# Upper and lower weight parts of the MLPs made per 2048-column unit in three buffers instead of per 1024-column half in six

## The chip, the cores and the metric

The kernel runs on one core of one Trainium2 chip. The metric is the device time of one execution in microseconds (us). A core has a matrix engine (PE, with its weight loads shown apart as PEld), a vector engine (DVE), an activation engine (ACT), GpSimd (POOL) and SyncE (SP), which here only issues transfers. Each engine works through its own queue in order. They wait for each other by semaphores.

## What is computed

The reference is a trunk of two layers on 256 tokens of width 2048, float32. Layer 0 mixes tokens by a convolution module, layer 1 by latent attention, and each mixer is followed by an MLP:

```
def sq_relu_mlp(h, w1, w2):
    return jnp.square(jax.nn.relu(h @ w1)) @ w2

for layer in range(DEPTH):
    h = rms_norm(x, norm_mixer_g[layer])
    x = x + (conv_module(h, ...) if layer % 2 == 0 else mla(h, ...))
    h = rms_norm(x, norm_mlp_g[layer])
    x = x + sq_relu_mlp(h, mlp_w1[layer], mlp_w2[layer])
return rms_norm(x, final_norm_g)
```

In the MLPs `w1` is 2048 x 8192 and `w2` 8192 x 2048, so their weights are 256 of the kernel's loads of 1 MB.

## The kernel before

**Products in two parts.** PE multiplies in a short float format (`F32R`). So each float32 operand is made into an upper part `hi`, a rounded copy, and a lower part `lo`, the rest, and a product is upper by upper, upper by lower and lower by upper. For weights, ACT writes `hi` (an activation with Copy, L443) and DVE then writes `lo = raw - hi` (a subtraction, L444). `lo` of a tile therefore always waits for `hi` of it. `split_into` (L442) issues both.

**The units of an MLP.** Each load of 128 x 2048 float32 into a tile `raw` is a unit. There are three kinds.
- An *up unit* ("T", `up_unit`, L515) is one block of 128 columns of `w1`. It is split as two halves of 1024 columns. PE runs 8 products with `hi` of the first half, 8 and 8 with `lo` of both halves, and 8 with `hi` of the second (L535 upper, 512 columns wide; L531 lower, 256 wide). Then ACT copies the result from PSUM to the tile `U` (L543).
- A *seven-product pair* ("S", `seven_unit`, L697) replaces the eight block products of two by two blocks of `w2` by seven, by Strassen's scheme in Winograd's form. DVE first makes four sums of the weight blocks: `T` (two at once, L735), and one after the other the two halves of `V` (L742, L747), the first from `T`, the second from the first. Four chunks follow: `one` (512 columns of `raw`), `two` (1024 of `raw`), `t13` (`T`), `t24` (`V`), each split and then used by 3 or 6 matmuls (L209, L210, L211).
- A *plain pair* ("O", `plain_unit`, L671) is two chunks of 1024 columns with 12 matmuls each.

**Activations of a pair.** When both up units (b = 0 and b = 1) of a pair are done, five steps are queued in a list `todo`: `add` (DVE, L558, the two halves of `U` added), an empty one, `square` (ACT: relu L563, then square L566), `forms` (DVE, three small subtractions L577, L580, L581) and `part` (ACT L443 writes `sh`, DVE L444 writes `sl`). The tiles are `W`, or `U` itself for a plain pair.

**The order.** `stream` (L446) writes out by hand, in the order of the program, what each engine does. Before chunk n is run on PE it prepares chunks up to n + 5 (`WB` = 6 buffers of 1024 columns for `hi`, six for `lo`). Ahead of each chunk that it prepares it takes one step from `todo`, or two if more than four are waiting (L459 to L479). The sums `T` are made one chunk earlier (`ahead`). An MLP has four parts (`q`). First come the 16 up units of part 0; then for parts 0 to 2 two stretches of 16 units each, in the orders `STSTSTOSTSTSTSTT` and `TSTSTSTOSTSTSTST` (L57), in which the pairs of one part and the up units of the next alternate; last, the 16 pairs of part 3 without up units. Here a *cycle* means the two stretches of one part: 14 S, 16 T and 2 O. There are six cycles in the kernel.

**Neighbours.** All stages share the `hi` and `lo` buffers of one pool, `wpool`; the convolution and the attention fill them through `split_half` (L168). The steps of the scheduler around an MLP are also of use below: `xs` adds (L362 and L609) put results onto the residual stream, `xt` (L224, L231) is the transposed input of the next products, and between the convolution and MLP 0 stands the preparation of the rotary tables: ACT issues the load of the positions (L1249), DVE works out the angles (L1251 to L1291), ACT takes sine and cosine (L1296, L1299).

Of the kernel before, what the change touches and what calls it, by code (L numbers as in the profile page):

```python
# [18 lines left out]
P = 128  # L19
D = 2048  # L20
KC = D // P
T = 2
# [18 lines left out]
LO_GAP = 64  # L41
# [4 lines left out]
WB = 6  # L46
LOOK = WB // 2 - 1
# [40 lines left out]
def trunk_kernel(  # L88
# [32 lines left out]
    small = ctx.enter_context(tc.tile_pool(name="small", bufs=1))  # L121
    psum, psum_cx = {}, [ExitStack()]
# [45 lines left out]
    def split_half(raw, h, eng):  # L168

        _, nj, cols = raw.shape  # L170
        js = slice(h * nj // 2, (h + 1) * nj // 2)
        hi = wpool.tile([P, nj // 2, cols], F32R, tag="hi", name=nm("hi"), bufs=WB)
        lo = wpool.tile([P, nj // 2, cols], F32R, tag="lo", name=nm("lo"), bufs=WB)
        nc.scalar.activation(hi, raw[:, js, :], AF.Copy)  # L174
        eng.tensor_tensor(lo, raw[:, js, :], hi.bitcast(F32), op=ALU.subtract)  # L175
        return hi, lo
# [256 lines left out]
    class Chunk:  # L433
        def __init__(self, prep, run, after=(), now=None, ahead=None):
            self.prep, self.run, self.after, self.now, self.ahead = prep, run, after, now, ahead
# [10 lines left out]
    def stream(chunks, todo, blocked, pool):  # L446
# [12 lines left out]
        def next_step():  # L459
            if todo and (todo[0] not in blocked or blocked[todo[0]]()):  # L460
                todo.pop(0)()

        def prep():
            n = done[0]
            if n == len(chunks):
                return
            done[0] += 1
            unit, c = chunks[n]
            unit.chunks[c].prep(raws[unit], parts.setdefault(unit, {}))
            if done[0] < len(chunks):  # L470
                unit, c = chunks[done[0]]
                if unit.chunks[c].ahead is not None:
                    unit.chunks[c].ahead(raws[unit])
                unit, c = chunks[n]
            if c == unit.last_read:
                start(homes[unit])
# [3 lines left out]
        for n, (unit, c) in enumerate(chunks):  # L480
            chunk = unit.chunks[c]
            while done[0] < min(n + WB, len(chunks)):
                for _ in range(2 if len(todo) > 4 else 1):
                    next_step()
                prep()
            if done[0] == len(chunks):
                for fn in todo[: 2 if n < len(chunks) - 1 else None]:
# [9 lines left out]
    def mlp(layer, ssq, next_gain, finish=None, before=None, last_w1=None):  # L497
# [11 lines left out]
        def up_units(hs, q, p, extra):  # L509
# [5 lines left out]
            def up_unit(b):  # L515
                ps = []

                def chunk(h):
                    def prep(raw, parts):
                        parts[h] = [a.rearrange("p a (j n) -> p (a j) n", n=P) for a in hi_lo(2, LO_GAP - 8)]  # L520
                        split_into(parts[h], raw[:, 8 * h : 8 * h + 8, :])

                    def run(parts):
                        if not ps:
                            ps.append(acc_tile())
                        wh, wl = parts.pop(h)
                        for low in (h, 1 - h):
                            for j in range(8):
                                k = 8 * h + j
                                if low:  # L530
                                    nc.tensor.matmul(  # L531
                                        ps[0][:, :S], wl[:, j, :], alternate(xh(k)), start=False, stop=False
                                    )
                                else:
                                    nc.tensor.matmul(  # L535
# [1301 lines left out]
```

## Time and profile before

| what | us |
|---|---|
| median of 3 runs (lowest, highest) | 1875.48 (1875.22, 1875.72) |
| the profiled execution's own time | 1875.54 |
| its span | 1873.8 |
| PE busy in the span | 1826.8 |
| DVE busy | 1645.1 |
| ACT busy | 1200.4 |

A span is the time from the first to the last instruction; the execution's own time is 1.7 us longer. In a timeline row stand the start and the duration in us, the engine, the source line, the operation, what it writes from what it reads, the shape, the count of like instructions merged into the row and, in brackets, how long the engine was idle before it and what ended that wait. Groups give the busy time and the mean duration of one in ns. Instructions of one engine overlap at their ends: the distance from one start to the next can be shorter than the duration.

### The profile page before, as it was taken

To read this page: it belongs to the slowest core of one execution; us is meant where nothing else is said; L and a number is where in the kernel's file an instruction comes from. 1 tells how busy PE (TensorE), PEld (TensorE's weight loads), DVE (VectorE), ACT (ScalarE), POOL (GpSimd) and SP (SyncE) were. 2 spreads that over 40 slices of the span, in tenths; PEclk is the share of its full clock that TensorE was granted. 3 is DMA by queue.
4 is the path that set the end of the run, shared out by engine and by line. 5 is a ranking of instruction groups with operands and counts; after the bars stand their busy time and mean duration, and the time that the engine had idled before them with its cause. 6 is when DMAs were issued, how large, how long until landed. Compare 5 with 4: busy or idle time off the path is not lost.

```text
span 1873.8 us, 28470 instructions
## 1 busy us (share of the span) xinstructions
PE 1826.8 (97%) x10768; PEld 1650.0 (88%) x10768; DVE 1645.1 (88%) x2370; ACT 1200.4 (64%) x1716; POOL 222.7 (12%) x185
## 2 busy tenths in 40 slices
PE   7999999999999999999999999999999999999998
PEld 7999888998888888888899998899888898888887
DVE  5999975789999999999977666668999999999987
ACT  5556764767666666767566665566666766666754
POOL 5999400000000000000001420000000000000000
PEclk9999999999999999999999999999999999999999
DMA  8767366857667667766646445776666776766763
GB/s 237 197 185 195 119 210 170 239 176 215 193 212 209 202 205 215 209 211 214 217 151 201 116 146 192 209 195 180 202 198 208 216 210 186 218 208 203 226 240 112
DMA packets 407113, 367.62 MB, mean 196 GB/s; under 512 B 15416, under 2 KB 351936, under 8 KB 406720
## 3 DMA queue, kind: packets, MB, share of 16 engines
q1 hardware_dynamic: 405952, 363.63, 64.9%
q8 instruction: 84, 1.38, 0.3%
q10 hardware_dynamic: 1024, 2.17, 0.3%
q14 instruction: 53, 0.43, 0.1%
HBM read 363.68 MB, written 2.10 MB: 195 GB/s over the span
## 4 chain that ended last, share of the span: by engine, by line
PE 70%; DVE 19%; ACT 5%; issue 4%; DMA 1%; POOL 0%; SPq 0%; ACTq 0%; DVEq 0%
PE acc L535 18%; PE acc L211 13%; PE acc L209 13%; PE acc L210 13%; PE acc L531 10%; DVE sum L996 7%; DVE lo L444 5%; ACT hi L443 2%; DVE lo L175 1%; DVE T L735 1%; PE acc L219 1%; PE acc L220 1%; PE acc L218 1%; PE acc L274 1%; DVE U L558 1%
## 5 line engine op out<-in xcount | busy, mean ns | idle before, releaser
L444 DVE TENSOR_TENSOR lo<-raw,hi 128x1024 fp32r<-128x1024 f32 (+1 forms) x512 | 569.8, 1121 | 65.9 <-ACT hi L443 65.5
L443 ACT ACTIVATE hi<-raw 128x1024 fp32r<-128x1024 f32 (+1 forms) x512 | 477.0, 968 | 46.1 <-PE acc L210 44.0
L535 PE MATMUL acc<-xt,hi 128*128 128x512 f32 x2048 | 478.2, 379 | 0.5 <-ACT hi L443 0.5
L535 PEld LDWEIGHTS acc<-xt,hi 128*128 128x128 f32 x2048 | 377.2, 189 | 48.7 <-ACT hi L443 0.9
L211 PE MATMUL acc<-lo,sh 128*128 128x512 f32 x930 | 355.4, 382 | 7.5 <-DVE lo L444 7.5
L209 PE MATMUL acc<-hi,sh 128*128 128x512 f32 x930 | 353.4, 380 | 0.0
L210 PE MATMUL acc<-hi,sl 128*128 128x512 f32 x802 | 304.0, 379 | 0.0
L531 PEld LDWEIGHTS acc<-xt,lo 128*128 128x128 f32 x2048 | 249.2, 192 | 11.0 <-DVE lo L444 4.2
L531 PE MATMUL acc<-xt,lo 128*128 128x256 f32 x2048 | 251.5, 275 | 2.7 <-DVE lo L444 2.1
L211 PEld LDWEIGHTS acc<-lo,sh 128*128 128x128 f32 x930 | 175.7, 189 | 43.0 <-DVE lo L444 18.2
L174 ACT ACTIVATE hi<-raw 128x1024 fp32r<-128x1024 f32 (+2 forms) x184 | 179.7, 1005 | 43.2 <-PE acc L210 39.4
L209 PEld LDWEIGHTS acc<-hi,sh 128*128 128x128 f32 x930 | 175.8, 189 | 23.7
L443 ACT ACTIVATE hi<-V 128x1024 fp32r<-128x1024 f32 x94 | 99.3, 1057 | 142.3 <-DVE V L747 133.0
L175 DVE TENSOR_TENSOR lo<-raw,hi 128x1024 fp32r<-128x1024 f32 (+2 forms) x118 | 132.7, 1144 | 63.2 <-ACT hi L174 63.0
L443 ACT ACTIVATE hi<-T 128x1024 fp32r<-128x1024 f32 x94 | 99.2, 1055 | 118.6 <-DVE T L735 107.0
L210 PEld LDWEIGHTS acc<-hi,sl 128*128 128x128 f32 x802 | 151.6, 189 | 21.5
L996 DVE SCALAR_TENSOR_TENSOR sum<-ub,w_dw,sum 128x256 f32<-128x256 f32 x392 | 159.1, 486 | 6.1 <-ACT sum L952 5.1
L175 POOL TENSOR_TENSOR lo<-raw,hi 128x1024 fp32r<-128x1024 f32 x66 | 156.6, 2387 | 22.7 <-ACT hi L174 20.6
L218 PE MATMUL acc<-xt,hi 128*128 128x256 f32 x512 | 142.2, 278 | 0.0
L219 PE MATMUL acc<-xt,hi 128*128 128x256 f32 x512 | 140.9, 275 | 0.5 <-DVE xt L231 0.5
L220 PE MATMUL acc<-xt,lo 128*128 128x256 f32 x512 | 141.0, 275 | 0.0
L444 DVE TENSOR_TENSOR lo<-V,hi 128x1024 fp32r<-128x1024 f32 x94 | 115.0, 1223 | 6.3 <-ACT hi L443 3.0
(275 smaller groups left out, 2760.2 us busy)
## 6 DMA issues: line engine op xcount, KB each, us to landing
raw<-in_mlp_w SPq DMA_DIRECT2D x256, 1024.0 KB, 6.1
raw<-in_conv_w_pw SPq DMA_DIRECT2D x64, 512.0 KB, 5.5
raw<-in_conv_w_pw SPq DMA_DIRECT2D x16, 1024.0 KB, 5.1
raw<-in_mla_w_o SPq DMA_DIRECT2D x16, 1024.0 KB, 5.5
raw<-in_mla_w_kv_up SPq DMA_DIRECT2D x8, 1024.0 KB, 5.4
raw<-in_mla_w_in SPq DMA_DIRECT2D x8, 576.0 KB, 3.8
raw<-in_mla_w_in SPq DMA_DIRECT2D x4, 1024.0 KB, 7.5
raw<-in_mla_w_q_up SPq DMA_DIRECT2D x16, 256.0 KB, 5.0
```

Source lines behind the costliest of these rows:

```text
L174: nc.scalar.activation(hi, raw[:, js, :], AF.Copy)
L175: eng.tensor_tensor(lo, raw[:, js, :], hi.bitcast(F32), op=ALU.subtract)
L209: nc.tensor.matmul(ps, sh, mh, start=start, stop=False)
L210: nc.tensor.matmul(ps, sl, mh, start=False, stop=False)
L211: nc.tensor.matmul(ps, sh, ml, start=False, stop=stop)
L218: nc.tensor.matmul(ps, wh, alternate(th), start=start, stop=False)
L220: nc.tensor.matmul(ps, wl, alternate(th), start=False, stop=stop)
L443: nc.scalar.activation(parts[0], src, AF.Copy)
L444: nc.vector.tensor_tensor(parts[1], src, parts[0].bitcast(F32), op=ALU.subtract)
L531: nc.tensor.matmul(ps[0][:, :S], wl[:, j, :], alternate(xh(k)), start=False, stop=False)
L535: nc.tensor.matmul(ps[0], wh[:, j, :], xhl(k).rearrange("p (g a b) -> p g b a", g=2, a=2), start=k == 0, stop=k == KC - 1,)
L996: nc.vector.scalar_tensor_tensor(out=out, in0=ubs[c][:, w : w + S], scalar=tap(c, w), in1=pcs[c], op0=ALU.mult, op1=ALU.add)
```

## The change

- `hi` and `lo` of an MLP have three buffers (`MB` = 3) of 2048 columns, in place of six of 1024. The total size is the same. They are taken from a pool of their own, closed and opened anew between the stages (`open_parts`), so that the first tiles of a stage lie over the last tiles of the stage before.
- An up unit and a plain pair are one chunk each: one ACT instruction and one DVE instruction of 2048 columns.
- A seven-product pair is two chunks: `alone` (1536 columns of `raw`) and `summed` (2048 columns). All four sums lie in one tile `TV`; `sums` makes the first three, `alone` the fourth.
- `stream` prepares chunks up to n + 2. It takes a batch of min(3, (length of `todo` + 1) // 2) steps ahead of each preparing function.
- The order of the matmuls is as it was. The shift of `lo` by `LO_GAP` is gone.

```
-    def hi_lo(n, at=0):
-        hi = wpool.tile([P, n, NB], F32R, tag="hi", name=nm("hi"), bufs=WB)
-        lo = wpool.tile([P, n * NB + LO_GAP], F32R, tag="lo", name=nm("lo"), bufs=WB)
-        return [hi, lo[:, at : at + n * NB].rearrange("p (a b) -> p a b", b=NB)]
+    def hi_lo(n):
+        return [
+            parts_pool[0].tile([P, 4, NB], F32R, tag=c, name=nm(c), bufs=MB)[:, :n, :] for c in ("hi", "lo")
+        ]
...
         def next_step():
-            if todo and (todo[0] not in blocked or blocked[todo[0]]()):
-                todo.pop(0)()
+            for _ in range(min(3, (len(todo) + 1) // 2)):
+                if todo and (todo[0] not in blocked or blocked[todo[0]]()):
+                    todo.pop(0)()

         def prep():
...
+            for i, fn in enumerate(unit.chunks[c].prep):
+                next_step()
+                fn(raws[unit], parts.setdefault(unit, {}))
+            if c == 0:
                 start(homes[unit])
...
-            while done[0] < min(n + WB, len(chunks)):
-                for _ in range(2 if len(todo) > 4 else 1):
-                    next_step()
+            while done[0] < min(n + MB, len(chunks)):
                 prep()
...
+                def prep(raw, parts):
+                    parts["w"] = hi_lo(4)
+                    split_into(parts["w"], raw.rearrange("p (a j) n -> p a (j n)", a=4))
...
+                def sums(raw, parts):
+                    x = raw.rearrange("p j (b n) -> p (j b) n", b=2)
+                    tv.append(mp.tile([P, 4, NB], F32, tag="TV", name=nm("TV"), bufs=1))
                     nc.vector.tensor_tensor(
+                        tv[0][:, 0:2, :], x[:, 0:1, :].broadcast_to([P, 2, NB]), x[:, 1:3, :], op=ALU.add
                     )
+                    nc.vector.tensor_tensor(tv[0][:, 2, :], tv[0][:, 0, :], x[:, 2, :], op=ALU.add)
+
+                def alone(raw, parts):
+                    x = raw.rearrange("p j (b n) -> p (j b) n", b=2)
+                    nc.vector.tensor_tensor(tv[0][:, 3, :], tv[0][:, 2, :], x[:, 3, :], op=ALU.add)
+                    parts["alone"] = hi_lo(3)
+                    split_into(parts["alone"], x[:, 1:4, :])
+
+                def summed(raw, parts):
+                    parts["summed"] = hi_lo(4)
+                    split_into(parts["summed"], tv[0])
...
+        open_parts(f"parts_m{layer}")
```

Three places show how the instructions move. In the changed program the lines are others: `split_into` is L452 (ACT) and L453 (DVE), the copy to `U` is L540, `add` L552, relu L557, square L560, `forms` L571 to L575, the sums L727, L730 and L734.

On ACT, in a stretch where S and T alternate, behind an up unit with b = 1, before:

```order
L443 ACTIVATE hi_6015<-raw_5864 128x1024
L543 ACTIVATE U_5946<-acc_5998 128x512
L443 ACTIVATE hi_6037<-raw_5864 128x1024
L563 ACTIVATE U_5946<-U_5946 128x2x256
L566 ACTIVATE W_6050<-U_5946 128x512
L443 ACTIVATE hi_6054<-raw_5887 128x512
```

The same place on ACT now (`hi_5918` is of the sums, `hi_5962` of the next up unit):

```order
L452 ACTIVATE hi_5918<-TV_5896 128x2048
L540 ACTIVATE U_5879<-acc_5922 128x512
L557 ACTIVATE U_5879<-U_5879 128x2x256
L560 ACTIVATE W_5958<-U_5879 128x512
L452 ACTIVATE hi_5962<-raw_5804 128x2048
```

Before, the `hi` that DVE needs next stood between the copy to `U` and the relu; now it stands behind relu and square.

On DVE, at the same place, before:

```order
L444 TENSOR_TENSOR lo_6016<-raw_5864,hi_6015 128x1024
L558 TENSOR_TENSOR U_5946<-U_5946 128x2x256
L444 TENSOR_TENSOR lo_6038<-raw_5864,hi_6037 128x1024
L735 TENSOR_TENSOR T_6041<-raw_5887 128x1024
L444 TENSOR_TENSOR lo_6055<-raw_5887,hi_6054 128x512
L742 TENSOR_TENSOR V_6042<-T_6041,raw_5887 128x512
```

And on DVE now, from the sums of a seven-product pair to the `forms`:

```order
L727 TENSOR_TENSOR TV_5896<-raw_5742 128x1024
L730 TENSOR_TENSOR TV_5896<-TV_5896,raw_5742 128x512
L734 TENSOR_TENSOR TV_5896<-TV_5896,raw_5742 128x512
L453 TENSOR_TENSOR lo_5901<-raw_5742,hi_5900 128x1536
L453 TENSOR_TENSOR lo_5919<-TV_5896,hi_5918 128x2048
L552 TENSOR_TENSOR U_5879<-U_5879 128x2x256
L453 TENSOR_TENSOR lo_5963<-raw_5804,hi_5962 128x2048
L571 TENSOR_TENSOR W_5958<-W_5958 128x256
```

Each sum now stands right behind the one that it reads; one instruction lies between the fourth sum and `lo` of the sums; and `lo_5963` follows the `add` with nothing between.

On DVE, at the passage from MLP 0 to the attention, before (`lo_9923` to `lo_9948` are of the first weights of the attention, 576 columns each):

```order
L175 TENSOR_TENSOR lo_9923<-raw_9916,hi_9922 128x576
L175 TENSOR_TENSOR lo_9927<-raw_9916,hi_9926 128x576
L175 TENSOR_TENSOR lo_9933<-raw_9918,hi_9932 128x576
L231 SCALAR_TENSOR_TENSOR xt_3456<-acc_9793,vecs,xt_3456 128x256 x2
L231 SCALAR_TENSOR_TENSOR xt_3456<-acc_9802,vecs,xt_3456 128x256 x2
L175 TENSOR_TENSOR lo_9937<-raw_9918,hi_9936 128x576
L231 SCALAR_TENSOR_TENSOR xt_3457<-acc_9827,vecs,xt_3457 128x256 x2
L231 SCALAR_TENSOR_TENSOR xt_3457<-acc_9836,vecs,xt_3457 128x256 x2
L175 TENSOR_TENSOR lo_9948<-raw_9920,hi_9947 128x576
L609 SCALAR_TENSOR_TENSOR xs<-acc_9593,r_480_3873,xs 128x512
```

And now:

```order
L603 SCALAR_TENSOR_TENSOR xs<-acc_8873,r_480_3876,xs 128x512
L603 SCALAR_TENSOR_TENSOR xs<-acc_8847,r_480_3876,xs 128x512
L603 SCALAR_TENSOR_TENSOR xs<-acc_8843,r_480_3876,xs 128x512
L603 SCALAR_TENSOR_TENSOR xs<-acc_8890,r_480_3876,xs 128x512
L1398 MEMSET scratch 64x256 x2
L1401 MEMSET scratch 1x64
L1402 MEMSET scratch 1x64
L1401 MEMSET scratch 1x64
L1402 MEMSET scratch 1x64
L184 TENSOR_TENSOR lo_9182<-raw_9175,hi_9181 128x576
```

The first `lo` of the attention (`lo_9923`, now `lo_9182`) stood ahead of the last four `xs` adds of the MLP, and stands behind them and the memsets now.

More of the change, by code (lines that the diff above doesn't have):

```diff
@@ L40 @@
 PAD_RIGHT = 40
-LO_GAP = 64
 PAD_XT = 16
@@ L46 @@
 WB = 6
+MB = 3
 LOOK = WB // 2 - 1
@@ L556, in add @@
+                after = [add, lambda: None, square, forms, part] + extra if b == 1 else []
+                return Unit(
+                    rows(w1, 0, KC, ((q * NPAIR + p) * 2 + b) * P, P), KC, [Chunk([prep], run, after)]
+                )
             def add():
@@ L737, in sums @@
                     )
-                def one(raw, parts):
-                    parts["one"] = hi_lo(1)
-                    split_into(parts["one"], x[0][:, 1:2, :])
-                    nc.vector.tensor_tensor(tt[1][:, 0, :], tt[0][:, 0, :], x[0][:, 2, :], op=ALU.add)
-                def two(raw, parts):
-                    parts["two"] = hi_lo(2)
-                    split_into(parts["two"], x[0][:, 2:4, :])
-                    nc.vector.tensor_tensor(tt[1][:, 1, :], tt[1][:, 0, :], x[0][:, 3, :], op=ALU.add)
```

161 lines of the change are left out of this document (65 added, 96 removed).

## The prediction

> **What bounds the kernel now.** I began with the page's first part, to see which engines are near their limit over the whole span.
>
> ```profile
> span 1873.8 us, 28470 instructions
> ...
> PE 1826.8 (97%) x10768; PEld 1650.0 (88%) x10768; DVE 1645.1 (88%) x2370; ACT 1200.4 (64%) x1716; POOL 222.7 (12%) x185
> ```
>
> PE is busy for 97%, so all the time to be won on it is 47 us; DVE follows with 88%. Means over unlike stages say little, so I went to one cycle (14 S, 16 T, 2 O), from the lower products of one up unit to those of the unit in the same place one part later.
>
> ```profile
> core 0: us, PE busy (x) PEld busy (x) DVE busy (x) ACT busy (x) POOL busy (x), PEclk, DMA share, GB/s
> 470.19:633.43 163.24, 160.17 (x856) 141.00 (x854) 158.67 (x185) 108.85 (x134) 0.00 (x0) 1.00 0.69 207
> ```
>
> A cycle lasts 163.24 us. DVE is busy for 158.67 of it and idle for 4.57, ACT for 67%. What PE needs at least follows from the chain that ended last, where two up units run without a wait.
>
> ```profile
> 628.35 1.78 PE acc L531 x16
> 630.13 3.46 PE acc L535 x16
> ```
>
> A matmul 512 wide takes a slot of 3.46/16 = 0.216 us, a lower one 1.78/16 = 0.111. An up unit is 16 and 16 of them, 5.24 us; a seven-product pair 21 x 0.216 = 4.54; a plain pair 24 x 0.216 = 5.18. A cycle is 16 x 5.24 + 14 x 4.54 + 2 x 5.18 = 157.8 us. DVE's 158.7 is as much: PE and DVE bound the cycle together, and every wait that DVE gets falls on the time. With T alone (the 16 units at an MLP's start) and in part 3 DVE has room. The groups, shapes apart, give the durations; behind the bar stands the idle time before them.
>
> ```profile
> L444 DVE TENSOR_TENSOR lo<-raw,hi 128x1024 fp32r<-128x1024 f32 x418 | 505.6, 1219 | 65.9 <-ACT hi L443 65.5
> L443 ACT ACTIVATE hi<-raw 128x1024 fp32r<-128x1024 f32 x418 | 432.4, 1046 | 43.0 <-PE acc L210 41.0 <-DVE W L637 1.5
> L444 DVE TENSOR_TENSOR lo<-raw,hi 128x512 fp32r<-128x512 f32 x94 | 64.3, 684 | 0.0
> L443 ACT ACTIVATE hi<-raw 128x512 fp32r<-128x512 f32 x94 | 58.1, 618 | 3.1 <-PE acc L210 3.1
> L558 DVE TENSOR_TENSOR U<-U 128x512 f32<-128x512 f32 x64 | 43.9, 687 | 10.7 <-ACT U L543 10.7
> L563 ACT ACTIVATE U<-U 128x512 f32<-128x512 f32 x64 | 40.1, 627 | 21.5 <-DVE U L558 21.5
> L566 ACT ACTIVATE W<-U 128x512 f32<-128x512 f32 x47 | 29.6, 631 | 1.5
> ```
>
> In a queue without waits the next instruction starts before the last has ended, unless it reads its result; the timeline shows by how much.
>
> ```profile
> 633.30 0.68 DVE L628 TENSOR_TENSOR W<-W,acc 128x512 f32<-128x512 f32 x1
> 634.01 0.69 DVE L629 TENSOR_TENSOR W<-W,acc 128x512 f32<-128x512 f32 x1
> 634.62 1.22 DVE L444 TENSOR_TENSOR lo<-raw,hi 128x1024 fp32r<-128x1024 f32 x1
> ...
> 639.56 0.68 DVE L636 TENSOR_TENSOR W<-acc,W 128x512 f32<-128x512 f32 x1
> 640.16 0.68 DVE L637 TENSOR_TENSOR W<-acc,W 128x512 f32<-128x512 f32 x1
> ...
> 646.99 2.35 DVE L444 TENSOR_TENSOR lo<-raw,hi 128x1024 fp32r<-128x1024 f32 x2
> ...
> 644.58 0.58 ACT L543 ACTIVATE U<-acc 128x512 f32<-128x512 f32 x1
> 645.05 2.52 ACT L443 ACTIVATE hi<-raw 128x1024 fp32r<-128x1024 f32 x3
> ```
>
> Two `lo` of 1024 in 2.35 us: starts 2.35 - 1.22 = 1.13 apart. Of 512: 640.16 - 639.56 = 0.60. So 512 columns more cost 0.53, and I take 1.66 for 1536 and 2.19 for 2048. Where the second reads the first's result (L628, L629), the starts are 0.71 apart, 0.11 more. On ACT the next starts 0.58 - 0.47 = 0.11 before the end.
>
> **DVE's own work** (per cycle). `lo` of a seven-product pair: before 3 x 1.13 + 0.60 = 3.99, now 1.66 + 2.19 = 3.85, 0.14 less. But the sums now stand behind each other: the third reads the first and always follows it directly, the fourth so follows the third in 66 of 94 places of the changed order. That is 0.11 + 0.08 more, in all +0.05 x 14 = +0.7. An up unit or plain pair: 2.26 before, 2.19 now, x 18 = -1.3. Together -0.6 us: half as many instructions on `lo`, and next to nothing gained.
>
> The Trainium skill (Perfetto Trace Analysis, Optimizing Scalar/DVE Operations) says that larger operations can help a saturated engine and puts a DVE instruction's fixed share at about 60 ns. The 350 DVE instructions dropped (2 x 94, 128 and 34) would by that be an estimated 21 us; the rows' 0.07 each agrees in size. The same section says that an engine that is not saturated but makes others wait is helped by smaller instructions. ACT, at 67% in the cycle, is such an engine, so by this rule the change goes the wrong way there.
>
> **The wait behind `add`.** By the changed order DVE's `add` is followed directly by `lo` of the next up unit. Its `hi` stands on ACT behind relu and square, and relu waits for that same `add`. The hand-overs are short.
>
> ```profile
> 329.16 0.69 DVE L558 TENSOR_TENSOR U<-U 128x512 f32<-128x512 f32 x1
> ...
> 329.88 0.64 ACT L563 ACTIVATE U<-U 128x512 f32<-128x512 f32 x1 [0.65 <-DVE U L558]
> ...
> 651.56 0.61 ACT L563 ACTIVATE U<-U 128x512 f32<-128x512 f32 x1
> 652.21 0.63 ACT L566 ACTIVATE W<-U 128x512 f32<-128x512 f32 x1
> ```
>
> From `add`'s end to the relu it is 329.88 - 329.85 = 0.03, from the relu's end to the square 652.21 - 652.17 = 0.04, and I take 0.03 from `hi` to `lo` too. So DVE stands idle for: the rest of `add` (0.69 - 0.60 = 0.09), 0.03 and the relu (0.63), 0.04 and the square (0.63 - 0.11 = 0.52), `hi` of 2048 columns and 0.03. No row has `hi` of 2048; two points give 1.046 + 2 x (1.046 - 0.618) = 1.90, with 1.7 and 2.1 (two of 1024) as bounds. That is 3.24, bounds 3.0 and 3.5. Before, this `hi` was issued ahead of the relu, so DVE went on. Nothing hides it: behind the waiting `lo` are queued `forms`, the next sums and every later `lo`. And PE has only `alone` and `summed` ahead, 4.53 us, against 0.58 (the copy to `U`) + 0.69 + 0.63 + 0.04 + 0.52 + 1.90 = 4.36 from the end of the up unit to the end of the next `hi`, without the handings over and only if DVE is free for `add` at once. By the changed order 6 of a cycle's 8 pairs stand so; at the other two that `hi` was issued earlier. 6 x 3.24 = 19.4 us.
>
> **The wait inside a seven-product pair.** The split of the sums waits for the fourth sum.
>
> ```profile
> 641.89 0.68 DVE L747 TENSOR_TENSOR V<-V,raw 128x512 f32<-128x512 f32 x1
> 642.66 1.06 ACT L443 ACTIVATE hi<-V 128x1024 fp32r<-128x1024 f32 x1 [4.04 <-DVE V L747]
> ```
>
> ACT starts 642.66 - 641.89 = 0.77 after the start of the last sum; with 1.90 and 0.03 `lo` can start 2.70 after it. DVE has only `lo` of 1536 to do meanwhile, 0.60 + 1.66 = 2.26: idle 0.44. Before, `lo` of `t13` stood there too. In 71 of 94 pairs nothing else lies between: 14 x 0.76 x 0.44 = 4.7 us. Behind the sums' `hi`, ACT copies to `U` (0.47) and does the next `hi` (1.90), 2.4 against DVE's 2.19: 0.2 at six places, 1.2.
>
> Of the 4.57 us that DVE was idle, most were waits for free buffers, which a late DVE doesn't have; I keep 1.5, with 0 and 4.57 as bounds: -3.1.
>
> A cycle changes by -0.6 + 19.4 + 4.7 + 1.2 - 3.1 = +21.6 us. Six cycles: +130. PE's 157.8 stays well below, so it doesn't limit.
>
> **The passages between stages.** The first tiles of MLP 0 lie over the convolution's last ones. So the first `hi` can start only at 305.17 us, where the fifth stood before, and the second and third come behind the end of the convolution, ahead of the load of the positions.
>
> ```profile
> 305.17 1.06 ACT L443 ACTIVATE hi<-raw 128x1024 fp32r<-128x1024 f32 x1 [1.53 <-PE acc L210]
> ...
> 311.59 0.40 ACTq L1249 DMA_DIRECT2D pos_i<-in_positions  x1
> ...
> 316.84 0.17 DVE L1251 CAST pos<-pos_i 128x2 f32<-128x2 int32 x1 [4.93 <-DMA pos_i<-in_positions]
> ...
> 324.22 0.26 ACT L1299 ACTIVATE cos<-an 128x64 f32<-128x64 f32 x1 [0.26 <-DVE an L1298]
> 324.38 1.04 ACT L443 ACTIVATE hi<-raw 128x1024 fp32r<-128x1024 f32 x1
> ...
> 325.47 0.70 PE L535 MATMUL acc<-xt,hi 128*128 128x512 f32 x2 [0.52 <-ACT hi L443]
> ```
>
> Two `hi` of 1.8 put the load at about 315.2 instead of 311.59. Landing, angles, sine and cosine take 12.6 us from there as before, so cosine ends near 328.0, and ACT waits for it in its queue. Then come the copy to `U` (0.47) and `hi` of 1.90, and PE, which has the three prepared units only, goes on near 330.4 instead of 325.47: +4.9. With 0.5 each for a late `lo` behind it and for the unit after: +6. At the passage to the attention DVE's first `lo` now stands behind the last `xs` adds.
>
> ```profile
> 961.24 2.72 DVE L609 SCALAR_TENSOR_TENSOR xs<-acc,r,xs 128x512 f32<-128x512 f32 x4 [0.68 <-PE acc L211]
> 964.07 0.55 DVE L1414 MEMSET scratch<- 64x256 f32 x2
> ...
> 965.07 2.10 DVE L175 TENSOR_TENSOR lo<-raw,hi 128x576 fp32r<-128x576 f32 x3
> ...
> 961.68 0.29 PE L209 MATMUL acc<-hi,xt 128*128 128x288 f32 x1
> ```
>
> PE went on at 961.68; its third product would now wait for a `lo` from 965.07 to 965.83: +4. At MLP 1's start `lo` stands behind the two `xs` adds, and at the end the last three pairs wait for whole buffers: an estimated +1 each, from the `hi` of 1.90 and the `lo` of 2.19 that are in part covered. Together +12, bounds 5 and 20.
>
> **The sum.** The span becomes 1873.8 + 130 + 12 = 2015.8, the time, with the 1.74 around the span in the profiled execution, 2017.5. The profiled execution (1875.54) stands by the median of the runs (1875.48). About 0.2% is what a measurement of this kernel can tell from no change.
>
> **The rivals.**
> - *Faster: grouping pays.* If the prepared buffers cover DVE's waits, PE's floor rules: 157.8 instead of 163.24 a cycle, 6 x -5.4 = -33, with the passages -21, 1854. For it: 4.57 us of idle DVE per cycle and a PE at its floor for long stretches. Against it: it decides itself at whether DVE has 3.24 us of other work between `add` and the next `lo`, and the order has none. The Trainium skill's grouping rule, taken alone, points here. Chance 0.03.
> - *Only the passages cost*: the cycles' waits and savings cancel, +12, 1887. It needs most of the 25 us of waits per cycle to fall on time that DVE had free, which is 4.57. Chance 0.03.
> - *Half of it*: the six waits fall partly on DVE's waits for PE, so that a cycle grows by 10 only: 60 and 12, 1947. Chance 0.13.
> - *PE and DVE take turns*: with two units ahead each waits for the other in the stretch TTT and at O, and all eight pairs of a cycle wait. Then -0.6 + 8 x 3.5 + 14 x 0.5 + 2.4 = 36.8 a cycle, +221, with 12 about 2108. Chance 0.11.
> - My sum: chance 0.70.
>
> **How the numbers follow.** The sum's own range: low, waits of 3.0, the two small ones gone, all idle time gone, 6 x (18.0 - 0.6 - 4.6) + 5 = +82, 1957; high, 3.5, no idle gone, 6 x (21.0 + 0.7 + 7.0 + 1.2) + 20 = +199, 2075. Half of it reaches just below the low end, so the range goes from 1945 to 2080. Slower by over 0.2% are all cases but the first, 0.97, less 0.01 that I leave to a result between; faster 0.03.
>
> **What would show it.** In the changed profile: a cycle of about 185 us; DVE's busy time in it near 158 but its share near 85%; in the waits, DVE `lo` for ACT `hi` as the longest by far, above 150 us in total with single waits near 3.3; PE waiting for ACT `hi` and DVE `lo` for over 100 us; `hi` of 2048 at 1.90 and `lo` at 2.29; near 308 to 330 us a PE wait of 5 to 6, and 4 where the attention begins. I am wrong if a cycle is under 165, if DVE's waits for `hi` are short, or if `hi` of 2048 is far from 1.90.

## The result and the profile after

The changed kernel takes 2016.43 us, the median of 6 runs (2016.20 to 2017.95), beside 1875.45 us for the kernel before (6 runs on the same chip). The ratio is 1.075 (95% interval 1.074 to 1.077), 141 us slower. The prediction was 2017.5 us, with a range from 1945 to 2080.

The page of the changed kernel, its first part:

```profile
span 2016.2 us, 27326 instructions
...
PE 1869.6 (93%) x10768; PEld 1653.1 (82%) x10768; DVE 1637.5 (81%) x2020; ACT 1167.2 (58%) x1366; POOL 222.5 (11%) x185
```

PE has gone from 97% to 93% and DVE from 88% to 81%. DVE's busy time is 7.6 us less and ACT's 33 less. PE has the same 10768 products and is busy for 43 us more. Part of that is how its time is recorded: a row of one product of 512 columns is 0.38 us long while the next starts 0.216 us after it, so each break in the run of products adds to the busy time. Some products also ran at half the clock, of which more below. So no work was added: the 142 us by which the span grew are waiting and slow products. The stages show where. The stretches of this view end with copies of up units to `U`: the 16th of MLP 0, its 64th, the first product of the attention with `kvh`, the 16th and the 64th of MLP 1, and the end. Columns: the stretch and its length, busy time of each engine, granted clock, share and rate of the transfers. First the kernel before:

```profile
0.00:393.97 393.97, 374.89 (x2663) 352.27 (x2664) 324.61 (x686) 240.21 (x380) 184.86 (x128) 1.00 0.68 194
393.97:881.14 487.17, 479.06 (x2563) 423.31 (x2562) 472.29 (x550) 327.01 (x402) 0.00 (x0) 1.00 0.69 206
881.14:1008.99 127.85, 127.85 (x698) 115.23 (x697) 111.26 (x165) 82.95 (x135) 0.11 (x1) 1.00 0.60 194
1008.99:1297.84 288.85, 285.94 (x1914) 265.86 (x1913) 193.24 (x329) 177.23 (x338) 37.73 (x56) 1.00 0.59 175
1297.84:1784.51 486.67, 478.80 (x2563) 423.39 (x2562) 471.76 (x548) 326.74 (x402) 0.00 (x0) 1.00 0.69 207
1784.51:1873.80 89.29, 80.25 (x372) 69.93 (x370) 71.98 (x95) 46.29 (x63) 0.00 (x0) 0.96 0.50 172
```

And the changed one:

```profile
0.00:397.96 397.96, 376.82 (x2663) 353.51 (x2664) 320.88 (x667) 237.03 (x361) 184.67 (x128) 1.00 0.67 190
397.96:945.39 547.43, 495.28 (x2563) 422.03 (x2562) 471.20 (x414) 315.35 (x263) 0.00 (x0) 0.99 0.62 184
945.39:1085.60 140.21, 133.37 (x699) 118.86 (x697) 112.75 (x145) 81.48 (x116) 0.11 (x1) 0.96 0.57 180
1085.60:1374.75 289.15, 286.17 (x1914) 265.93 (x1913) 189.10 (x310) 173.79 (x319) 37.70 (x56) 1.00 0.58 171
1374.75:1920.97 546.22, 495.18 (x2563) 421.96 (x2562) 470.02 (x411) 314.80 (x264) 0.00 (x0) 0.99 0.62 185
1920.97:2016.20 95.23, 82.74 (x372) 70.83 (x370) 73.53 (x78) 44.79 (x46) 0.00 (x0) 0.95 0.50 166
```

The two long stretches with three cycles each grew by 60.3 and 59.6 us. The other four grew by 4.0, 12.4, 0.3 and 5.9. Now a cycle, between the same points as in the prediction (there 163.24 us, DVE busy for 158.67), and the waits of DVE in it, as total, count and longest:

```profile
490.15:672.32 182.17, 163.74 (x855) 139.55 (x854) 157.99 (x139) 104.94 (x88) 0.00 (x0) 1.00 0.62 185
```

```profile
DVE lo L453 <- ACT hi L452: 22.8, 16, 3.2
```

A cycle lasts 182.17 us, 18.9 more. DVE works for 157.99 of it, 0.7 less than before, and stands idle for 24.2. Of that, 22.8 us are waits of `lo` for `hi`. The timeline of DVE shows both kinds, one inside a pair between its two `lo`, one behind `add` (L552):

```profile
581.29 1.75 DVE L453 TENSOR_TENSOR lo<-raw,hi 128x1536 fp32r<-128x1536 f32 x1
583.45 2.29 DVE L453 TENSOR_TENSOR lo<-TV,hi 128x2048 fp32r<-128x2048 f32 x1 [0.41 <-ACT hi L452]
585.66 0.69 DVE L552 TENSOR_TENSOR U<-U 128x512 f32<-128x512 f32 x1
589.50 2.29 DVE L453 TENSOR_TENSOR lo<-raw,hi 128x2048 fp32r<-128x2048 f32 x1 [3.16 <-ACT hi L452]
```

And ACT at the same place:

```profile
581.49 1.93 ACT L452 ACTIVATE hi<-TV 128x2048 fp32r<-128x2048 f32 x1 [3.65 <-DVE TV L734]
584.26 0.60 ACT L540 ACTIVATE U<-acc 128x512 f32<-128x512 f32 x1 [0.84 <-PE acc L529]
586.38 0.63 ACT L557 ACTIVATE U<-U 128x512 f32<-128x512 f32 x1 [1.52 <-DVE U L552]
587.04 0.63 ACT L560 ACTIVATE W<-U 128x512 f32<-128x512 f32 x1
587.58 1.89 ACT L452 ACTIVATE hi<-raw 128x2048 fp32r<-128x2048 f32 x1
```

`add` ends at 586.35, relu starts at 586.38, the square follows, then 1.89 us of `hi`, and DVE can go on at 589.50. The bracket of that row gives 3.16 us of idle time. In the cycle such a wait of 3.16 stands six times (five times ahead of `lo` of an up unit or plain pair, once ahead of `lo` of the sums) and a wait of 0.37 to 0.41 ten times: 19.0 and 3.9 of the 22.8. The durations that the prediction had to extrapolate are in the groups, shapes apart:

```profile
L453 DVE TENSOR_TENSOR lo<-raw,hi 128x2048 fp32r<-128x2048 f32 x162 | 370.2, 2289 | 129.8 <-ACT hi L452 128.8
...
L452 ACT ACTIVATE hi<-raw 128x2048 fp32r<-128x2048 f32 x162 | 306.4, 1902 | 42.1 <-PE acc L219 41.3 <-PE acc L220 0.4
```

`hi` of 2048 takes 1.90 us as predicted, `lo` 2.29. In the whole kernel 129.8 us of DVE's idle time stand in front of these 162 `lo` alone.

### The profile page after: what moved, and what is told of

Read it like the earlier page. It is cut to its first block, busy times and chain, and to the rows that moved or that the text cites. A ratio compares the mean times of both kernels' runs of the same rounds, so it can differ in the third digit from the quotient of the medians.

```text
span 2016.2 us, 27326 instructions
## 1 busy us (share of the span) xinstructions
PE 1869.6 (93%) x10768; PEld 1653.1 (82%) x10768; DVE 1637.5 (81%) x2020; ACT 1167.2 (58%) x1366; POOL 222.5 (11%) x185
## 3 DMA queue, kind: packets, MB, share of 16 engines
q10 hardware_dynamic: 1024, 2.17, 0.3%
## 4 chain that ended last, share of the span: by engine, by line
DVE 40%; PE 37%; ACT 13%; issue 9%; DMA 1%; POOL 0%; ACTq 0%; DVEq 0%
DVE lo L453 14%; ACT hi L452 8%; PE acc L220 8%; PE acc L218 8%; PE acc L219 8%; DVE sum L979 7%; PE acc L529 7%; DVE TV L727 4%; PE acc L536 4%; DVE TV L730 2%; DVE xs L603 2%; DVE TV L734 2%; DVE U L552 2%; ACT U L557 1%; DVE sl L453 1%
## 5 line engine op out<-in xcount | busy, mean ns | idle before, releaser
L453 DVE TENSOR_TENSOR lo<-raw,hi 128x2048 fp32r<-128x2048 f32 (+1 forms) x256 | 534.9, 2092 | 129.8 <-ACT hi L452 128.8
L452 ACT ACTIVATE hi<-raw 128x2048 fp32r<-128x2048 f32 (+1 forms) x256 | 441.0, 1746 | 49.4 <-PE acc L219 48.6
L220 PE MATMUL acc<-lo,sh 128*128 128x512 f32 x930 | 364.3, 392 | 65.5 <-DVE lo L453 65.2
L452 ACT ACTIVATE hi<-TV 128x2048 fp32r<-128x2048 f32 x94 | 180.3, 1918 | 268.8 <-DVE TV L734 265.1
L453 DVE TENSOR_TENSOR lo<-TV,hi 128x2048 fp32r<-128x2048 f32 x94 | 215.3, 2291 | 50.4 <-ACT hi L452 50.4
L540 ACT ACTIVATE U<-acc 128x512 f32<-128x512 f32 x128 | 75.7, 592 | 133.1 <-PE acc L529 128.4
```

The costliest lines, as they stand in the source:

```text
L220: nc.tensor.matmul(ps, sh, ml, start=False, stop=stop)
L452: nc.scalar.activation(parts[0], src, AF.Copy)
L453: nc.vector.tensor_tensor(parts[1], src, parts[0].bitcast(F32), op=ALU.subtract)
```

## The experiments

The kernel before ran beside each of these kernels, in 1875.2 to 1875.5 us. For the cycle I use one stretch in all runs, from the copy of the 32nd up unit of MLP 0 to that of the 48th: 163.24 us before (558.63 to 721.87), 182.17 in the changed kernel (584.26 to 766.43).

### The slot ends behind `add`

```
+    def pause():
+        pass
...
-                    todo.pop(0)()
+                    step = todo.pop(0)
+                    step()
+                    if step is pause:
+                        return
...
-                after = [add, lambda: None, square, forms, part] + extra if b == 1 else []
+                after = [add, pause, square, forms, part] + extra if b == 1 else []
```

> The changed kernel with one edit to the pace of its steps: the empty step behind `add` ends the slot, so that relu and square come one slot later, behind the next `hi`. Buffers, units and splits stay as changed. Theory (the steps' batches): DVE's six waits of 3.16 us per cycle go, 19.0 us, so a cycle falls from 182.2 to about 163.5 and the time from 2016.4 by 6 x 19.0 = 114 to about 1902 (1890 to 1925); of DVE's waits for `hi` only the short ones of 0.4 within the pairs stay. Rival (the units of 2048 themselves, with three buffers, are too coarse): the wait moves to the next `hi` of 1.9 us and the time stays at 1980 or above.

1915.4 us (1911.2 to 1915.6, 4 runs; ratio to before 1.021, 1.019 to 1.022). Moving relu and square one slot later takes 101 us of the 141 away, with the units, the splits, the buffers and the pools as changed. The cycle and DVE's waits in it:

```profile
568.15:734.40 166.25, 160.34 (x855) 140.73 (x854) 158.34 (x139) 104.76 (x87) 0.00 (x0) 1.00 0.67 203
```

```profile
DVE lo L453 <- ACT hi L452: 6.4, 17, 0.6
```

In this stretch the changed kernel has 23.3 us of such waits; now they are 6.4, the longest 0.6. So the six waits of 3.16 came from the batch. Four of them fell to 0.35 to 0.59 and not to nothing: there ACT does the next `hi` directly behind the copy to `U`, and its 1.9 us are longer than what DVE has left to do. The other two fell to 0.10 and to nothing. Within the cycle 15.9 us came back and not 19.0. The rival, that the wait moves on to the next coarse `hi` at its full length, is out.

### The sums split in halves

```
-                    split_into(parts["summed"], tv[0])
+                    for at in (0, 2):
+                        split_into([a[:, at : at + 2, :] for a in parts["summed"]], tv[0][:, at : at + 2, :])
```

> The changed kernel with the split of the four sums made in two instructions of 1024 columns on each engine instead of one of 2048, in the same buffer. Theory: the first half's `hi` waits for the third sum only and is done early, so the 0.4 us that DVE waits in a pair go at 10 of 14 pairs, -4.0 per cycle; 14 more `lo` cost 14 x 0.07 = 1.0; -3 per cycle, 6 x -3 = -18, about 1998 (1992 to 2004). The waits of 3.16 stay. Rival (grouping saves fixed time on DVE, and its short waits would be spent elsewhere anyway): 14 more `lo` a cycle cost 1.0 and nothing is won, about 2022.

1993.4 us (1992.3 to 1994.7, 4 runs; ratio 1.063, 1.061 to 1.065), 23 less than the changed kernel; 19 of that lie in the cycles and 5 in the last parts of the MLPs. The waits of 0.4 are gone, and the rival with them. Of the waits of `lo` only those behind `add` are left in the cycle:

```profile
DVE lo L453 <- ACT hi L452: 18.1, 6, 3.2
```

This one cycle fell by 1.7 us only, from 182.17 to 180.43 (581.53 to 761.96); the mean of the six is 3.2. In it stand three new waits of `add` for the copy to `U`, 1.02 us each, and three spells of 3.41 us in which PE ran at half the clock. The whole execution has sixteen spells at half the clock ahead of its last microseconds, the changed kernel eight.

### Both

> Both edits: the slot that ends behind `add`, and the sums' split in two halves. Theory: 2016.4 - 114 - 18 = 1884, a cycle of about 160.5, still above the kernel before because of what lies outside the cycles (28 us between the two kernels). Rival, if the cycle is bound by PE's wait for whole units once DVE's are gone: the second edit gains nothing on top of the first, 1900 or above.

1892.9 us (4 runs within 0.1; ratio 1.009, 1.008 to 1.011). Neither forecast is met to the letter: 9 us above the theory, 7 below the rival's bound. The second edit gains 22.4 us on top of the first, and 23 without it, so the two waits are separate. The cycle is that of the kernel before again:

```profile
563.15:726.58 163.43, 159.71 (x855) 140.97 (x854) 157.97 (x153) 107.39 (x101) 0.00 (x0) 1.00 0.68 206
```

Of the 17.4 us that are left, 16 lie outside the cycles.

### The kernel before with the new pace

```
         def next_step():
-            if todo and (todo[0] not in blocked or blocked[todo[0]]()):
-                todo.pop(0)()
+            for _ in range(min(3, (len(todo) + 1) // 2)):
+                if todo and (todo[0] not in blocked or blocked[todo[0]]()):
+                    todo.pop(0)()
...
-                for _ in range(2 if len(todo) > 4 else 1):
-                    next_step()
+                next_step()
```

> The kernel before with nothing but the changed kernel's rule for the steps (one call ahead of each chunk, up to three steps in it); parts of 1024 in six buffers, sums and splits as before. By its order `add` is followed by a `lo` whose `hi` stands behind relu and square at the same 6 of 8 pairs of a cycle. Theory (the steps' batches): the wait is that of the changed kernel less the shorter `hi`, 3.16 - (1.90 - 1.05) = 2.3, six times 13.9, less the 3.1 us of old idle time, +10.8 per cycle, 6 x 10.8 = 65, about 1940 (1925 to 1955). Rival (the units of 2048 are the cause, six finer buffers cover such waits): 1885 or less.

1950.0 us (1948.7 to 1950.4, 4 runs; ratio 1.040, 1.038 to 1.041). The rule for the steps alone, with small parts in six buffers, makes the old kernel 75 us slower. DVE behind `add`:

```profile
575.54 0.68 DVE L558 TENSOR_TENSOR U<-U 128x512 f32<-128x512 f32 x1
578.53 1.23 DVE L444 TENSOR_TENSOR lo<-raw,hi 128x1024 fp32r<-128x1024 f32 x1 [2.30 <-ACT hi L443]
```

The wait is 2.30 us, 2.3 was expected: relu, square and one `hi` of 1024. It stands six times in the cycle.

### Small splits in the changed kernel, with its batches and without

In both, each split of 1536 or 2048 columns is made in two instructions per engine, in the changed kernel's tiles:

```
-                    split_into(parts["w"], raw.rearrange("p (a j) n -> p a (j n)", a=4))
+                    for at in (0, 2):
+                        split_into([a[:, at : at + 2, :] for a in parts["w"]],
+                                   raw.rearrange("p (a j) n -> p a (j n)", a=4)[:, at : at + 2, :])
```

Plain pairs and sums go likewise, `alone` as 512 and 1024. With the batches as changed:

> The changed kernel with all splits in instructions of 1024 or 512, and its steps in batches as changed (`add`, relu and square in one slot). Theory (the wait behind `add` is relu, square and one `hi`, whatever the buffers): six waits of 3.16 - 0.85 = 2.3 us a cycle, 13.9, stand on top of the cycle of 161.3 of the run with small splits and steps apart: 1876.3 + 6 x 13.9 = 1960 (1950 to 1970). Rival (small instructions alone cure it): 1900 or less.

1960.8 us (1958.5 to 1961.8, 4 runs; ratio 1.045, 1.044 to 1.047).

```profile
DVE lo L453 <- ACT hi L452: 13.8, 6, 2.3
```

Six waits, 13.8 us in all, 13.9 expected. With the slot that ends behind `add`:

> The changed kernel with the slot that ends behind `add` and with every split made in instructions of 1024 or 512 columns; units and three buffers of 2048 stay. So it has the instruction sizes of the kernel before with the buffers of the changed one. Theory (coarse buffers cost at the passages only, what costs in the cycle is the length of one `hi` and where it stands): DVE's own work 157.97 + 18 x 0.07 + 14 x 0.07 = 160.2 a cycle, idle 5.5 - 3 = 2.5, a cycle of 162.7 and about 1889 (1884 to 1893). Rival (three whole units in flight hold DVE and ACT up while PE has not released one): a cycle of 165 or more, 1900 or above.

1876.3 us (1876.0 to 1877.7, 11 runs; ratio 1.001, 1.000 to 1.002): no difference from the kernel before, and 13 us less than the theory's number, below its range. The rival is out. Its cycle:

```profile
557.29:718.59 161.30, 159.87 (x855) 140.86 (x854) 159.70 (x185) 110.35 (x134) 0.00 (x0) 1.00 0.69 209
```

161.30 us with 159.70 of DVE work. DVE is idle for 1.6, where I had expected 2.5, and its work is 0.5 below what I had worked out. The changed kernel's buffers and units thus cost nothing in the cycle; they make it 1.9 us shorter than before.

### The pools, in the kernel before

```
-        hi = wpool.tile([P, n, NB], F32R, tag="hi", name=nm("hi"), bufs=WB)
+        hi = parts_pool[0].tile([P, n, NB], F32R, tag="hi", name=nm("hi"), bufs=WB)
...
+        open_parts(f"parts_m{layer}")
```

> The kernel before, its parts of 1024 in six buffers, steps and splits as they were, but with the parts' pool closed and opened anew at each stage, as the changed kernel does. Theory P (the passages between the stages pay for the pools: a stage's first parts lie over the last ones of the stage ahead): +4 at the start of the first MLP and +6.5 at the start of the attention, as in the run with both edits, about 1886 (1882 to 1890). Rival Q (the passages pay for whole units: instructions of 2048 and three buffers, whatever pool they lie in): 1878 or less.

1900.2 us (1898.9 to 1901.3, 4 runs; ratio 1.013, 1.012 to 1.015). The direction is theory P's, the size is more than twice it. The attention starts 6.8 us later than before, and MLP 1 4.7. At the start of MLP 0 it is 14.4. The cycle is as before (163.23 us). PE there:

```profile
308.75 0.88 PE L283 MATMUL acc<-ident,xs 128*128 128x128 f32 x6 [0.21 <-DVE xs L371]
321.52 2.07 PE L544 MATMUL acc<-xt,hi 128*128 128x512 f32 x4 [11.90 <-ACT hi L452]
```

And ACT:

```profile
310.24 0.83 ACT L233 ACTIVATE xt<-acc,vecs 128x256 fp32r<-128x256 f32 x2
319.61 0.26 ACT L1306 ACTIVATE sin<-an 128x64 f32<-128x64 f32 x1 [8.54 <-DVE an L1301]
319.77 0.24 ACT L1307 ACTIVATE an<-an 128x64 f32<-128x64 f32 x1
320.27 0.26 ACT L1309 ACTIVATE cos<-an 128x64 f32<-128x64 f32 x1 [0.26 <-DVE an L1308]
320.43 6.72 ACT L452 ACTIVATE hi<-raw 128x1024 fp32r<-128x1024 f32 x7
```

With the tiles tied to the end of the convolution, all `hi` of MLP 0 have come to stand behind the cosine, seven in a row from 320.43. In the kernel before six stood ahead of it, from 294.81 on, and in the changed kernel three do. PE's first products behind its wait are slow as well: the granted clock was 0.50 from 313.49 to 327.14, and the four products in the row above take 2.07 us. So the pools alone cost, and how much hangs on which `hi` still comes ahead of the tables.

### Six tiles in one pool, and the fourth sum apart

The kernel with small splits, with its `hi` and `lo` in the old pool for the whole program, six tiles of 1024 each; a unit takes two:

```
+    def split_pair(src):
+        made, n = [], src.shape[1]
+        for at, to in ((0, n - 2), (n - 2, n)):
+            made.append([
+                wpool.tile([P, 2, NB], F32R, tag=c, name=nm(c), bufs=WB)[:, : to - at, :] for c in ("hi", "lo")
+            ])
+            split_into(made[-1], src[:, at:to, :])
+        return made
```

> The changed kernel with the slot that ends behind `add`, small splits, and six tiles of 1024 in the weights' old pool for the whole program instead of three of 2048 in a pool for each stage; units stay whole and three ahead. Theory (coarse buffers and pools cost at the passages, nothing in the cycles): the cycles of the run with small splits, 161.3 instead of 163.24, with the passages of the kernel before: 1875.4 - 6 x 1.9 = 1864 (1860 to 1868). Rival (the finer release of tiles changes nothing at the passages, since whole units wait there anyway): 1874 to 1877.

1867.3 us (1867.2 to 1867.5, 5 runs; ratio 0.996, 0.995 to 0.997). The cycle is again 161.30. From the 64th up unit to the attention it takes 127.85 us, as before. The 9 us between the two runs all lie at the passages. The run changed the pool and the tile size together, so how the 9 divide between them isn't settled. Then the fourth sum was put between the two splits of `alone`:

```
-                    parts["alone"] = split_pair(x[:, 1:4, :])
+                    parts["alone"] = split_pair(x[:, 1:4, :], lambda: nc.vector.tensor_tensor(
+                        tv[0][:, 3, :], tv[0][:, 2, :], x[:, 3, :], op=ALU.add
+                    ))
```

> The run with six tiles, and the fourth sum between the two splits of the first chunk, so that it no longer stands directly behind the third. Theory (DVE sets the cycle, and a result read by the very next instruction costs it 0.1 us): 14 x 0.1 = 1.4 a cycle less than with six tiles alone, 6 x 1.4 = 8 us, about 1856. Rival (PE's floor of 157.8 with its own waits sets it now): the same as with six tiles alone within 2.

1863.5 us (1863.5 to 1863.8, 5 runs; ratio 0.994, 0.992 to 0.995), the fastest of all, 11.7 us below the kernel before.

```profile
555.33:715.84 160.51, 159.19 (x855) 141.18 (x854) 158.88 (x185) 110.10 (x133) 0.00 (x0) 1.00 0.71 210
```

The gain is 3.8 us, half of the 8 expected. The cycle and DVE's work both fell by 0.8 us (161.30 to 160.51, 159.70 to 158.88), so DVE still has a part in setting it, though PE is busy for as long (159.19). The work fell by 0.8 and not by 1.4 because in the run ahead the fourth sum stood directly behind the third at 10 of the cycle's 14 pairs only, and each of these gained 0.08 of busy time.

### Products added in PE's idle time

```
                     banks[name] = acc_tile()
+                if not filled:
+                    filled.append(True)
+                    for _ in range(20):
+                        nc.tensor.matmul(
+                            banks[name], sh, xhl(0).rearrange("p (g a b) -> p g b a", g=2, a=2), start=True, stop=True
+                        )
```

> The changed kernel with 20 products of 512 columns added on PE ahead of the first product of a seven-product pair in each MLP, into the bank that this product then clears; nothing else. PE stood idle there for 3.33 and 1.18 us and then ran 13 products with slots of 0.43 us instead of 0.216 (PEclk 0.67 in that stretch); the added ones take 20 x 0.216 = 4.3 us in the idle time. Theory (the idle time itself brings the half clock, and PE is what is late there): the slow spell goes, 13 x 0.21 = 2.8 us at the first MLP and about as much at the second, 2016.4 - 5 = 2011 (2009 to 2013). Rival (DVE is late there and covers PE's slow spell, or the spell comes anyway): 2016.4 within 1.

2012.7 us (2011.3 to 2014.1, 4 runs; ratio 1.073, 1.072 to 1.075), 3.8 less than the changed kernel, by work that was added. The 20 products ran one pair and one up unit ahead of the idle time (397.87 to 402.35) and pushed PE's later work into it. In the changed kernel, behind waits of 3.33 and 1.18 us, PE's products start 0.43 us apart instead of 0.216:

```profile
412.18 0.48 PE L218 MATMUL acc<-hi,sh 128*128 128x512 f32 x1 [3.33 <-ACT hi L452]
412.50 0.38 PE L219 MATMUL acc<-hi,sl 128*128 128x512 f32 x1
414.06 0.79 PE L220 MATMUL acc<-lo,sh 128*128 128x512 f32 x1 [1.18 <-DVE lo L453]
414.64 0.63 PE L218 MATMUL acc<-hi,sh 128*128 128x512 f32 x1
415.07 0.63 PE L219 MATMUL acc<-hi,sl 128*128 128x512 f32 x1
```

The same stretch of time in both kernels, changed and filled; behind the five busy times stands the granted clock, 0.50 and 1.00:

```profile
413.30:420.12 6.82, 6.06 (x14) 4.87 (x15) 6.42 (x5) 4.81 (x4) 0.00 (x0) 0.50 0.50 159
```

```profile
413.30:420.12 6.82, 5.51 (x24) 4.54 (x25) 6.45 (x4) 4.80 (x4) 0.00 (x0) 1.00 0.49 157
```

The slow spell is gone. In this execution the filled kernel is ahead by 1.6 us at the 24th up unit of MLP 0, and the same stretch of MLP 1 wins 1.2: of the 5 us expected at the two places, 2.8 came. In both rows DVE is busy for 6.4 of the 6.8 us. So DVE is late there too, and I put the missing half down to it, which is argued and not shown. The two profiled executions (2017.95 and 2011.35 us) are further apart than the medians: 4.0 us of the difference lie between the last up unit of MLP 0 and the attention, where the edit adds nothing and this execution had no slow spell.

### One `lo` on GpSimd

```
-    def split_into(parts, src):
+    def split_into(parts, src, eng=nc.vector):
...
-        nc.vector.tensor_tensor(parts[1], src, parts[0].bitcast(F32), op=ALU.subtract)
+        eng.tensor_tensor(parts[1], src, parts[0].bitcast(F32), op=ALU.subtract)
...
-                    split_into(parts["two"], x[0][:, 2:4, :])
+                    split_into(parts["two"], x[0][:, 2:4, :], nc.gpsimd)
```

> The kernel before with one `lo` of each seven-product pair (1024 columns, the chunk with two parts) on the idle GpSimd instead of DVE. If PE and DVE bound the cycle of the kernel before together, DVE's work falls by 14 x 1.13 = 15.8 to 142.9 a cycle and PE's floor of 157.8 is left: 163.24 to about 159, 6 x -4 = -25, about 1850 (1843 to 1860), faster than both kernels. Rival (a `lo` on GpSimd, 2.38 us in the convolution, comes too late for PE or slows DVE by sharing): 1875 or above.

1963.9 us (1963.6 to 1966.1, 4 runs; ratio 1.047, 1.046 to 1.049), 88 us slower. DVE and GpSimd at one such place:

```profile
605.46 1.08 DVE L444 TENSOR_TENSOR sl<-W,sh 128x896 fp32r<-128x896 f32 x1
606.47 2.85 DVE L444 TENSOR_TENSOR lo<-raw,hi 128x512 fp32r<-128x512 f32 x1
609.24 0.68 DVE L742 TENSOR_TENSOR V<-T,raw 128x512 f32<-128x512 f32 x1
```

```profile
605.86 2.90 POOL L444 TENSOR_TENSOR lo<-raw,hi 128x1024 fp32r<-128x1024 f32 x1 [13.16 <-ACT hi L443]
```

A `lo` of 512 columns, 0.68 us elsewhere, takes 2.85 on DVE: it starts at 606.47 while GpSimd is at work and ends 0.56 after GpSimd does (608.76). The load taken off DVE comes back as stretched instructions; its busy time in the cycle rose from 158.67 to 171.81. The other half of the rival, that such a `lo` comes too late for PE, hardly shows: in the cycle PE waited for one once, 0.3 us. The Trainium skill (SBUF — State Buffer, Who interferes with whom) says that a DVE instruction with two inputs in SBUF contends with a GpSimd instruction that reads SBUF, and calls the lock on the pair of ports that they share exclusive. This trace agrees: 2.85 us in place of 0.68.

## Why the prediction was right, and which steps were not

**The wait behind `add`: right.** 3.16 us against 3.24, at 6 of 8 pairs. Undoing the batch alone gave 101 us back, and the batch alone in the old kernel cost 75. That `hi` of 2048 is part of its length is shown by small splits with the batches kept: 3.16 became 2.3.

**The wait inside a pair: right, a little smaller than forecast.** 0.4 at ten pairs, 3.9 us, against 4.7. Halving the sums' split removed it.

**DVE's own work: right.** 0.7 us less against 0.6.

**The copy to `U` and the `hi` behind it: not there.** Of the 24.2 us idle, 19.0 and 3.9 are the two waits. The 1.3 left over are what I kept of the old idle time (1.5). The 1.2 us for this step don't show.

So a cycle came to +18.9 against +21.6, six of them to 114 against 130.

**The passages: the step that failed.** "Together +12, bounds 5 and 20" stands there. What lies outside the cycles is 142.4 - 113.6 = 28.8 us, above the upper bound. The total came out within 1 us because this error and that of the cycles, +17 and -16, cancel. That is luck, though the time would have lain inside the range with either error alone. By places:
- Start of MLP 0: 4.0 against 6. PE went on at 327.85 and not at 330.4, behind a wait of 2.74 us where 5 to 6 was given as a sign. The load of the positions left ACT's queue at 313.71, while the third `hi` was still running (313.56 to 315.50). I had put it behind that `hi`.

```profile
313.56 1.94 ACT L452 ACTIVATE hi<-raw 128x2048 fp32r<-128x2048 f32 x1
313.71 0.40 ACTq L1232 DMA_DIRECT2D pos_i<-in_positions  x1
```

- Start of the attention: the wait of PE was 3.59 us, against 4. But the whole stretch from the last up unit grew by 12.4. Of that, the pairs ahead of it hold 3.3 us more of PE's waits (0.77, 1.63 and 0.86 behind `hi` and `lo` of whole units). I had said of part 3 that DVE has room; for a unit as a whole it has not.
- The end: 5.9 against 1, with 3.5 us of the same kind of waits (0.77, 1.63, 1.09).
- The first stretches behind the 16 up units: 3.5 and 2.8 us over three cycles of 18.9, for which I had nothing. Of these, 2.7 and 2.4 lie in the first of the three cycles.
- No term at all stood for the clock, and no reason for leaving it out. Spells at half clock followed the longer waits of PE. There are eight ahead of the last microseconds, 37.5 us in all, and none lies in the steady cycle of 182.17: one at the start of MLP 0, two in the first cycle of each MLP, two between the last up unit of MLP 0 and the attention, one behind the last up unit of MLP 1. Half the clock costs at most half of a spell, which makes an estimate of up to 18.8 of the 28.8 us. In the stretch from the last up unit of MLP 0 there are 3.41 and 6.83 us of them. If half of that is lost it is 5.1, and the 12.4 less the waits of 6.9 leaves 5.5. The run with added products shows this cost for one place in each MLP; for the others it is argued from these numbers only.

The rivals fell by the cycle: it is neither at PE's floor of 157.8, nor unchanged, nor at 173, nor at 200. Of the Trainium skill's two rules that the prediction weighed (Perfetto Trace Analysis, Optimizing Scalar/DVE Operations), the one on smaller instructions for an engine that is not saturated but makes others wait held: with the steps apart, small splits took the changed kernel from 1915.4 to 1876.3. What the rule on grouping saved, DVE's 159.70 less 158.34 us in these two cycles, is real and 1.4 us. In the whole changed kernel DVE's busy time fell by 7.6 us, where the prediction's estimate from the rule was 21.

In one chain: 2016.4 changed; 1915.4 with relu and square a slot later; 1876.3 with small splits; 1867.3 with six tiles in one pool; 1863.5 with the fourth sum apart. What of the change pays, 1.9 us a cycle once the other costs are gone, is in what was left of it: the plan by whole units, the sums in one tile, the steps in batches that end behind `add`. Which of these, wasn't tried.

## What to carry to other kernels

When two engines work in step and one waits for the other's result, look at what stands in the queue between the result asked for and the engine that makes it: one slot of the plan that held `add`, relu and square together cost 101 us, though no instruction was added. Group the bookkeeping (buffers, units of the plan) if you like, but keep the instruction short that another engine waits for, and keep a pool open over a stage's end if the next stage is to start early. And price a wait of PE of about 2 us or more with the slow products that can follow, not with its length alone.

## What the runs showed of the hardware

- The granted clock fell to exactly one half in spells of 3.41 us or a multiple (6.83 in several runs, 13.65 once, in the run with the pools). The kernel before has none ahead of its last microseconds; the changed one has eight. In one execution the starts of the spells stand whole multiples of 3.413 us apart: in the changed kernel 327.97, 413.30, 467.92 and 952.61, which is 25, 16 and 142 times. A full 3.41 us of idle time isn't needed. In the run with halved sums one wait of 1.91 us (568.29 to 570.20) lay in the first of these two stretches:

```profile
567.37:570.78 3.41, 1.50 (x8) 0.99 (x7) 3.41 (x4) 3.29 (x5) 0.00 (x0) 1.00 0.64 184
570.78:574.19 3.41, 3.41 (x10) 2.69 (x9) 3.41 (x3) 2.56 (x2) 0.00 (x0) 0.50 0.85 262
```

PE was busy for 1.50 of 3.41 us at full clock, and in the next 3.41 the clock was 0.50. In the changed kernel's own cycle (PEclk 1.00 in the row above) PE's longest wait is as long, and the clock didn't fall:

```profile
PE acc L220 <- DVE lo L453: 12.4, 12, 1.9
```

There a wait of 1.91 us, 571.99 to 573.90, lies across a border of that grid (573.73), and in the 3.41 us ahead of the border PE was busy for 1.67. Cut along their grids, from 12 us on, the thirteen traces give this: each of the 30 windows at full clock with PE busy for 43% or less was followed by half clock, none of the 7089 with 53% or more was, and 29 of the 69 in between were. What decides in between isn't settled. The Trainium skill (TensorE: Matmul & The Clock Gate, HAM oscillation — how this bites in real kernels) gives the rule that PE should have no idle gaps of more than about 3.4 us; here one of 1.91 was enough.
- The issue of a transfer on ACT's queue doesn't wait for the end of the ACT instruction ahead of it (changed kernel: 313.71, inside 313.56 to 315.50).
